# A mean-subtraction kernel on a ring of SBUF slots: blocks of three groups per partition, moved in two DMAs of 50,688 bytes a partition

## The chip, the cores and the metric

The kernel runs on one core of a Trainium2 chip. The metric is the device time of one execution in microseconds (us), lower is better. Each profile below is one execution; its span is about 1.8 us shorter than the time that is measured for it. A run counts as slow when it lies over 1.5% above the fastest of the same kernel.

## The reference

```python
B, S, D = 8, 4096, 2112          # float32
stride = 4
x_r = x.reshape(B, S // stride, stride, D)
pooled = x_r.mean(axis=2)
return x - np.repeat(pooled, stride, axis=1)
```

From every four adjacent rows their mean is subtracted. There are 8192 groups of four rows. A group has 4 x 2112 values, 33,792 bytes, and is contiguous in memory. Every byte must be read once and written once: 553.65 MB in all. That makes the kernel a copy with a little arithmetic in the middle.

## The kernel before

128 groups make a tile, one group in each partition. Six slots in SBUF (the memory on the chip that DMAs fill and engines work on) each hold one tile. SP (the sync engine's queue) issues loads, DVE (the vector engine) does three additions and one multiply-and-add, ACT's queue issues stores. All waits are set by hand on semaphores, counters that a finished DMA or instruction raises. A load into a slot waits only for the store that left that slot six tiles earlier. The words "group" and "tile" are used alike below for these 128 groups: there are 64 of them in the run.

```python
SLOTS = 6
PAD = 224
...
    pad_pool.tile([P, PAD], f32, name="pad")          # 896 bytes, never used
    slots = [io_pool.tile([P, W], f32, name=f"slot{b}") for b in range(SLOTS)]
...
        for k in range(n):                            # n = 64
            b, lap = k % SLOTS, k // SLOTS
            rows = slots[b].rearrange("p (f d) -> p f d", f=STRIDE)
            s = s_ps if k % 2 else s_sb
            tile_rows = slice(k * P, (k + 1) * P)

            load = nc.sync.dma_start(out=slots[b][:], in_=xg[tile_rows])
            if lap:
                load._wait_ge(store_sems[b], 16 * lap)
            load.then_inc(load_sems[b], 16)

            add = nc.vector.tensor_add(out=s[:], in0=rows[:, 0, :], in1=rows[:, 1, :])
            add._wait_ge(load_sems[b], 16 * (lap + 1))
            ...                                       # two more additions, one subtraction
            store = nc.scalar.dma_start(out=og[tile_rows], in_=slots[b][:])
            store._wait_ge(done_sem, done)
            store.then_inc(store_sems[b], 16)
```

Of the kernel before, what the change touches and what calls it, by code (L numbers as in the profile page):

```python
# [1 line left out]

# [4 lines left out]

STRIDE = 4
SLOTS = 6  # L10
PAD = 224


@with_exitstack
def kernel(
    ctx: ExitStack,
    tc: tile.TileContext,
    x: bass.AP,
    out: bass.AP,
):  # L20





    nc = tc.nc
    B, S, D = x.shape
    P = nc.NUM_PARTITIONS
    W = STRIDE * D
    G = (B * S) // STRIDE  # L30
    assert S % STRIDE == 0 and G % P == 0
    n = G // P

    xg = x.rearrange("b (g f) d -> (b g) (f d)", f=STRIDE)
    og = out.rearrange("b (g f) d -> (b g) (f d)", f=STRIDE)
    f32 = mybir.dt.float32

    pad_pool = ctx.enter_context(tc.tile_pool(name="pad", bufs=1))
    io_pool = ctx.enter_context(tc.tile_pool(name="io", bufs=1))
    sum_pool = ctx.enter_context(tc.tile_pool(name="sum", bufs=1))  # L40
    psum_pool = ctx.enter_context(
        tc.tile_pool(name="psum", bufs=1, space=bass.MemoryType.PSUM)
    )
    pad_pool.tile([P, PAD], f32, name="pad")
    slots = [io_pool.tile([P, W], f32, name=f"slot{b}") for b in range(SLOTS)]
    s_sb = sum_pool.tile([P, D], f32, name="s_sb")
    s_ps = psum_pool.tile([P, D], f32, name="s_ps")

    load_sems = [tc.alloc_semaphore(f"load{b}") for b in range(SLOTS)]
    store_sems = [tc.alloc_semaphore(f"store{b}") for b in range(SLOTS)]  # L50
    done_sem = tc.alloc_semaphore("done")

    with tc.tile_critical():  # L53
        done = 0
        for k in range(n):
            b, lap = k % SLOTS, k // SLOTS
            rows = slots[b].rearrange("p (f d) -> p f d", f=STRIDE)
            s = s_ps if k % 2 else s_sb
            tile_rows = slice(k * P, (k + 1) * P)

            load = nc.sync.dma_start(out=slots[b][:], in_=xg[tile_rows])
            if lap:
                load._wait_ge(store_sems[b], 16 * lap)
            load.then_inc(load_sems[b], 16)

            add = nc.vector.tensor_add(out=s[:], in0=rows[:, 0, :], in1=rows[:, 1, :])  # L66
            add._wait_ge(load_sems[b], 16 * (lap + 1))
            add.then_inc(done_sem)
            done += 1
            for f in range(2, STRIDE):  # L70
                add = nc.vector.tensor_add(out=s[:], in0=s[:], in1=rows[:, f, :])  # L71
                add._wait_ge(done_sem, done)
                add.then_inc(done_sem)
                done += 1
            sub = nc.vector.scalar_tensor_tensor(  # L75
                out=rows,
                in0=s[:, None, :].to_broadcast([P, STRIDE, D]),
                scalar=-1.0 / STRIDE,
                in1=rows,
                op0=mybir.AluOpType.mult,  # L80
                op1=mybir.AluOpType.add,
            )
            sub._wait_ge(done_sem, done)
            sub.then_inc(done_sem)
            done += 1

            store = nc.scalar.dma_start(out=og[tile_rows], in_=slots[b][:])
            store._wait_ge(done_sem, done)
            store.then_inc(store_sems[b], 16)

        for b in range(SLOTS):
            nc.sync.wait_ge(store_sems[b], 16 * len(range(b, n, SLOTS)))


# [1 line left out]
_INS = ['x']  # L96
_OUTS = [((8, 4096, 2112), 'float32')]


# [23 lines left out]
```

## Time and profile before

| | kernel before |
|---|---|
| median of 6 runs | 1286.87 us (1286.72 to 1287.26) |
| span of the profiled run | 1285.0 us |
| DVE busy | 1026.5 us, 16.1 us a group |
| data moved | 553.67 MB, mean 431 GB/s |
| DMA packets an engine | 1024 rows of 33,792 bytes |

These are lines of the profile page of the kernel before. The two rows of the second part cut the span into 40 slices: DMA is the busy share of the 16 DMA engines in tenths, GB/s what they moved, loads and stores together.

```profile
span 1285.0 us, 439 instructions
DVE 1026.5 (80%) x256; POOL 0.2 (0%) x4
...
DMA  9999999999999999999999999999999999999998
GB/s 404 421 438 432 426 438 437 430 429 437 437 431 429 437 437 431 429 437 437 431 429 437 437 431 429 437 436 430 430 438 434 429 432 438 434 428 433 438 434 374
DMA packets 18434, 553.67 MB, mean 431 GB/s; under 512 B 2048, under 2 KB 2048, under 8 KB 2048
```

The 2048 small packets, 4 bytes and 9 ns each in the packet records, are 16 for each of 128 DMAs; I take them for the semaphore updates. The view by windows of the same run gives, for each stretch, its length, the busy time of DVE and POOL with the number of their instructions, the clock share, the DMA share and GB/s:

```profile
100.00:500.00 400.00, 321.20 (x81) 0.00 (x0) 1.00 1.00 433
500.00:1150.00 650.00, 523.49 (x130) 0.00 (x0) 1.00 1.00 433
...
1265.00:1270.00 5.00, 4.57 (x1) 0.00 (x0) 1.00 1.00 433
1270.00:1277.00 7.00, 0.00 (x0) 0.00 (x0) 1.00 1.06 459
```

The DMA share is 1.00 in every stretch from 50 to 1270 us (0.98 in the first 50): the engines hardly pause before the end. The view of waits says what DVE waits for (us in total, times, longest):

```profile
DVE s_sb L66 <- DMA slot<-in_x_dram: 123.4, 30, 13.3
DVE s_ps L66 <- DMA slot<-in_x_dram: 113.0, 30, 4.8
```

60 waits, all for loads, 236 us in all. So DMA is the bound and DVE has slack of about 3.8 us a group (16.1 of 19.95 us). The timeline has the last arithmetic:

```profile
1253.41 2.37 DVE L66 TENSOR_TENSOR s_ps<-slot 128x2112 f32<-128x2112 f32 x1 [3.82 <-DMA slot<-in_x_dram]
1255.81 4.77 DVE L71 TENSOR_TENSOR s_ps<-s_ps,slot 128x2112 f32<-128x2112 f32 x2
1260.61 8.96 DVE L75 SCALAR_TENSOR_TENSOR slot<-s_ps,slot 128x8448 f32<-128x8448 f32 x1
```

The last store leaves at 1269.6 us. At that time the engines are still writing the store before it, which lands at 1273.4 us. There is no gap.

### The profile page before, as it was taken

The page shows a single profiled execution, that of the slowest core. Times are in us where ns is not written, and L with a number is a line of the kernel's source. Part 1 is how long each engine was busy: PE and PEld are TensorE (multiplying, and loading weights), DVE is VectorE, ACT ScalarE, POOL GpSimd, SP SyncE. Part 2 cuts the span into 40 slices and gives each one's busy share as a digit, 9 for nine tenths or more (in the row PEclk, how much of TensorE's full clock was granted, in tenths as well). Part 3 has the DMA queues.
Part 4 walks back from the last instruction along what each step waited for, and adds up shares of the span by engine and source line. Part 5 has one row for each costly group of instructions (what it writes and reads, how often), then busy time and mean ns, then how long its engine had stood idle before and what let it go on. Part 6 is the DMA issues. An engine that isn't in the chain of part 4 may idle for free.

```text
span 1285.0 us, 439 instructions
## 1 busy us (share of the span) xinstructions
DVE 1026.5 (80%) x256; POOL 0.2 (0%) x4
## 2 busy tenths in 40 slices
DVE  5998778787787877878778788787887878878774
POOL 0000000000000000000000000000000000000000
DMA  9999999999999999999999999999999999999998
GB/s 404 421 438 432 426 438 437 430 429 437 437 431 429 437 437 431 429 437 437 431 429 437 437 431 429 437 436 430 430 438 434 429 432 438 434 428 433 438 434 374
DMA packets 18434, 553.67 MB, mean 431 GB/s; under 512 B 2048, under 2 KB 2048, under 8 KB 2048
## 3 DMA queue, kind: packets, MB, share of 16 engines
q1 hardware_dynamic: 9216, 276.83, 50.0%
q10 hardware_dynamic: 9216, 276.83, 49.9%
q14 instruction: 2, 0.02, 0.0%
HBM read 276.82 MB, written 276.82 MB: 431 GB/s over the span
## 4 chain that ended last, share of the span: by engine, by line
DVE 80%; another core or an unknown queue 17%; DMA 1%; issue 0%; SPq 0%
DVE slot L75 45%; DVE s_ps L71 12%; DVE s_sb L71 12%; DVE s_ps L66 6%; DVE s_sb L66 6%; DMA slot<-in_x_dram 1%; SPq L118 0%; SPq L53 0%
## 5 line engine op out<-in xcount | busy, mean ns | idle before, releaser
L75 DVE SCALAR_TENSOR_TENSOR slot<-s_sb,slot 128x8448 f32<-128x8448 f32 x32 | 286.7, 8958 | 1.1
L75 DVE SCALAR_TENSOR_TENSOR slot<-s_ps,slot 128x8448 f32<-128x8448 f32 x32 | 286.6, 8957 | 1.1
L66 DVE TENSOR_TENSOR s_sb<-slot 128x2112 f32<-128x2112 f32 x32 | 75.5, 2358 | 123.4 <-DMA slot<-in_x_dram 123.4
L66 DVE TENSOR_TENSOR s_ps<-slot 128x2112 f32<-128x2112 f32 x32 | 75.7, 2367 | 113.0 <-DMA slot<-in_x_dram 113.0
L71 DVE TENSOR_TENSOR s_ps<-s_ps,slot 128x2112 f32<-128x2112 f32 x64 | 151.4, 2366 | 2.2
L71 DVE TENSOR_TENSOR s_sb<-s_sb,slot 128x2112 f32<-128x2112 f32 x64 | 150.9, 2358 | 2.2
L107 POOL MEMSET const-uint8-127<- 128x1 uint8 x1 | 0.1, 102 | 0.0
L107 POOL MEMSET const-bfloat16-1.0<- 128x1 bf16 x1 | 0.1, 101 | 0.0
L107 POOL MEMSET const-float32-0.0<- 128x1 f32 x1 | 0.1, 98 | 0.2 <-issue 0.2
L107 POOL MEMSET const-float32-1.0<- 128x1 f32 x1 | 0.1, 98 | 0.0
## 6 DMA issues: line engine op xcount, KB each, us to landing
slot<-in_x_dram SPq DMA_DIRECT2D x64, 4224.0 KB, 59.7
out_dram<-slot ACTq DMA_DIRECT2D x64, 4224.0 KB, 43.9
```

Source lines behind the costliest of these rows:

```text
L66: add = nc.vector.tensor_add(out=s[:], in0=rows[:, 0, :], in1=rows[:, 1, :])
L71: add = nc.vector.tensor_add(out=s[:], in0=s[:], in1=rows[:, f, :])
L75: sub = nc.vector.scalar_tensor_tensor(out=rows, in0=s[:, None, :].to_broadcast([P, STRIDE, D]), scalar=-1.0 / STRIDE, in1=rows, op0=mybir ...
L107: nc = _bacc.Bacc("TRN2", target_bir_lowering=False, num_devices=1)
```

## The change

The intent: fewer and larger DMA packets. A partition now owns three adjacent groups, 101,376 contiguous bytes, moved as two DMAs of 50,688 bytes a partition. The six slots become one ring that holds two such blocks. 20 blocks of three are followed by four single groups. The pad tile goes. Eight semaphores a side serve in turn. The core of the diff:

```diff
-SLOTS = 6
-PAD = 224
+RING = 6
+SUPER = 3
+TAIL = 4
+SEMS = 8
...
+    blocks = [SUPER] * ((n - TAIL) // SUPER)
+    blocks += [1] * (n - sum(blocks))
+    for k in blocks:
+        src = xg[rows].rearrange("(p j) w -> p (j w)", j=k)
+        dst = og[rows].rearrange("(p j) w -> p (j w)", j=k)
+        parts = 1 if k == 1 else 2
+        step = k * W // parts
+        for h in range(parts):
+            ...  # moves: ring columns, source, destination, last group that the move holds
+        for j in range(k):
+            ...  # groups: ring column, last move that must have landed
-    pad_pool.tile([P, PAD], f32, name="pad")
-    slots = [io_pool.tile([P, W], f32, name=f"slot{b}") for b in range(SLOTS)]
+    ring = io_pool.tile([P, RING * W], f32, name="ring")
...
+        for i, (a, b, src, _, _) in enumerate(moves):
+            taken = ...  # stores whose ring columns this load overwrites
+            load = nc.sync.dma_start(out=ring[:, a:b], in_=src)
+            for m in taken[-1:]:
+                load._wait_ge(*landed(store_sems, m))
...
+            while stored < len(moves) and moves[stored][4] <= j:
+                a, b, _, dst, _ = moves[stored]
+                store = nc.scalar.dma_start(out=dst, in_=ring[:, a:b])
```

Two things follow. The middle group of a block lies in both halves, so the first half can be stored only after the second half has landed and two groups are done. And the ring now has four pieces in flight instead of six.

More of the change, by code (lines that the diff above doesn't have):

```diff
@@ L30 @@
     G = (B * S) // STRIDE
-    assert S % STRIDE == 0 and G % P == 0
+    assert S % STRIDE == 0 and G % P == 0 and (SUPER * W) % 2 == 0
     n = G // P
+    f32 = mybir.dt.float32
     xg = x.rearrange("b (g f) d -> (b g) (f d)", f=STRIDE)
     og = out.rearrange("b (g f) d -> (b g) (f d)", f=STRIDE)
-    f32 = mybir.dt.float32
-    pad_pool = ctx.enter_context(tc.tile_pool(name="pad", bufs=1))
+    blocks = [SUPER] * ((n - TAIL) // SUPER)
+    blocks += [1] * (n - sum(blocks))
+    moves = []
+    groups = []
+    slot = g0 = 0
+    for k in blocks:
+        assert slot + k <= RING
+        rows = slice(g0, g0 + k * P)
+        src = xg[rows].rearrange("(p j) w -> p (j w)", j=k)
+        dst = og[rows].rearrange("(p j) w -> p (j w)", j=k)
+        parts = 1 if k == 1 else 2
+        step = k * W // parts
+        first_move, first_group = len(moves), len(groups)
+        for h in range(parts):
+            part = slice(h * step, (h + 1) * step)
+            a = slot * W + h * step
+            last = first_group + ((h + 1) * step - 1) // W
+            moves.append((a, a + step, src[:, part], dst[:, part], last))
+        for j in range(k):
+            groups.append(((slot + j) * W, first_move + ((j + 1) * W - 1) // step))
+        g0 += k * P
+        slot = (slot + k) % RING
     io_pool = ctx.enter_context(tc.tile_pool(name="io", bufs=1))
@@ L43, with landed @@
     )
-    pad_pool.tile([P, PAD], f32, name="pad")
-    slots = [io_pool.tile([P, W], f32, name=f"slot{b}") for b in range(SLOTS)]
+    ring = io_pool.tile([P, RING * W], f32, name="ring")
     s_sb = sum_pool.tile([P, D], f32, name="s_sb")
     s_ps = psum_pool.tile([P, D], f32, name="s_ps")
-    load_sems = [tc.alloc_semaphore(f"load{b}") for b in range(SLOTS)]
-    store_sems = [tc.alloc_semaphore(f"store{b}") for b in range(SLOTS)]
+    load_sems = [tc.alloc_semaphore(f"load{i}") for i in range(SEMS)]
+    store_sems = [tc.alloc_semaphore(f"store{i}") for i in range(SEMS)]
     done_sem = tc.alloc_semaphore("done")
+    def landed(sems, i):
+        return sems[i % SEMS], 16 * (i // SEMS + 1)
     with tc.tile_critical():
-        done = 0
-        for k in range(n):
-            b, lap = k % SLOTS, k // SLOTS
-            rows = slots[b].rearrange("p (f d) -> p f d", f=STRIDE)
-            s = s_ps if k % 2 else s_sb
-            tile_rows = slice(k * P, (k + 1) * P)
-            load = nc.sync.dma_start(out=slots[b][:], in_=xg[tile_rows])
-            if lap:
-                load._wait_ge(store_sems[b], 16 * lap)
-            load.then_inc(load_sems[b], 16)
+        owner = {}
+        free = set()
+        for i, (a, b, src, _, _) in enumerate(moves):
+            taken = sorted(
+                {m for (p, q), m in owner.items() if p < b and a < q} - free
+            )
+            for m in taken[:-1]:
+                nc.sync.wait_ge(*landed(store_sems, m))
+            load = nc.sync.dma_start(out=ring[:, a:b], in_=src)
+            for m in taken[-1:]:
+                load._wait_ge(*landed(store_sems, m))
+            load.then_inc(load_sems[i % SEMS], 16)
+            free.update(taken)
+            owner = {c: m for c, m in owner.items() if m not in free}
+            owner[(a, b)] = i
+        done = 0
+        seen = -1
+        stored = 0
+        for j, (c, need) in enumerate(groups):
+            rows = ring[:, c:c + W].rearrange("p (f d) -> p f d", f=STRIDE)
+            s = s_ps if j % 2 else s_sb
             add = nc.vector.tensor_add(out=s[:], in0=rows[:, 0, :], in1=rows[:, 1, :])
-            add._wait_ge(load_sems[b], 16 * (lap + 1))
+            assert need <= seen + 1
+            if need > seen:
+                add._wait_ge(*landed(load_sems, need))
+                seen = need
             add.then_inc(done_sem)
@@ L85 @@
             done += 1
-            store = nc.scalar.dma_start(out=og[tile_rows], in_=slots[b][:])
-            store._wait_ge(done_sem, done)
-            store.then_inc(store_sems[b], 16)
-        for b in range(SLOTS):
-            nc.sync.wait_ge(store_sems[b], 16 * len(range(b, n, SLOTS)))
+            while stored < len(moves) and moves[stored][4] <= j:
+                a, b, _, dst, _ = moves[stored]
+                store = nc.scalar.dma_start(out=dst, in_=ring[:, a:b])
+                store._wait_ge(done_sem, done)
+                store.then_inc(store_sems[stored % SEMS], 16)
+                stored += 1
+        assert stored == len(moves)
+        for m in sorted(set(range(len(moves))) - free):
+            nc.sync.wait_ge(*landed(store_sems, m))
 _INS = ['x']
```

## The prediction

> **What bounds the kernel now: the 16 DMA engines, throughout.** The page shows a span of 1285.0 us (timed: 1286.73), DVE busy 1026.5 us (80%), and 553.67 MB at a mean of 431 GB/s. The view by windows gives 433 GB/s and a DMA share of 1.00 from 50 to 1260 us. The view of waits has DVE waiting 236 us for loads, for nothing else. The trace's packet records sharpen this: a packet is one partition's row of 33,792 bytes; rows follow each other every 1247.8 ns on each engine without a gap, from about 1.95 to 1281.5 us. 1024 rows x 1.2478 us = 1278 us: that is the kernel; some 2 us at each end are the rest. The chain of waits names DVE for 80%, but DVE works 16.1 us of each 19.95 us, so it is not the bound.
>
> [...]
>
> **What the change does.**
> - Removes: data packets per engine fall from 1024 to 704 (640 of 50,688 bytes), DMAs from 128 to 88. [...] about 0.4 us of semaphore packets (9 ns each). [...]
> - Adds, silently: the pad tile is gone. In the built programs the slots began at an SBUF address that is a multiple of 512; the ring and all its moves begin 128 bytes past one. [...]
> - Moves: the first addition starts near 18 us instead of 13.3; the first store leaves only after group 1, near 50 us instead of 29.5. Six groups of loads keep the engines busy until about 60 us, so this costs nothing. DVE work is the same 256 instructions.
> - Tail: before, the last store was issued at 1269.6 us with about 2 us of backlog. A small queue model fitted to the trace gives an idle gap of 0 to 3 us just before the last single store; I count 1 us.
> - Middle: loads are issued in bursts, but the model always keeps work in one of the two queues.
>
> **Sum:** [...] All of it is on the critical path, which is the DMA engines.
>
> **Prediction: 1286.0 us, 8 in 10 between 1283.0 and 1291.0. Chances: faster by over 2% 0.01, within 2% 0.94, slower by over 2% 0.05.**
>
> **What would show it.** 11,264 data packets[...]. DMA share 1.00 in the middle; any drop near 1270 us only. DVE busy unchanged, with fewer, longer waits for loads.
>
> **What would make it wrong.** [...] Landings later than modelled would empty both queues once per block and cost 10 to 30 us.

The forecast's sum came to +0.9 us over the timed 1286.73: -0.4 for the semaphore packets, +1 for the tail, and two terms, a saving by fewer data packets and the cost of the start address ("alignment" below), which came to about +0.3 together. For doubt of the second it was then shaded down to 1286.0.

## The result, and the profile after

The changed kernel took 1289.56 us (median of 6: 1290.40, 1286.27, 1286.33, 1288.72, 1292.78, 1293.20). The kernel before took 1286.87. The ratio of the fast runs is 1.0021, with a 95% interval of 0.9999 to 1.0042: the same. Ratios here are the mean time of one kernel's fast runs over the mean of the other's in the same rounds, so they are not quite the ratio of the medians. The new thing is the spread: 7 us, against 0.5 us before. The profiled run is the one of 1290.40 us. Its page:

```profile
span 1288.6 us, 398 instructions
DVE 1023.0 (79%) x256; POOL 0.2 (0%) x4
...
DMA  9999999999999999999999999999999999999997
GB/s 403 428 428 434 439 436 428 428 439 437 431 430 434 441 433 428 433 439 434 431 431 439 436 431 430 437 438 431 430 434 442 431 430 431 437 437 425 429 428 325
DMA packets 12674, 553.67 MB, mean 430 GB/s; under 512 B 1408, under 2 KB 1408, under 8 KB 1408
```

Its waits and its windows:

```profile
DVE s_sb L103 <- DMA ring<-in_x_dram: 132.0, 11, 18.8
DVE s_ps L103 <- DMA ring<-in_x_dram: 114.3, 11, 12.4
```

```profile
50.00:100.00 50.00, 49.69 (x14) 0.00 (x0) 1.00 1.00 424
100.00:500.00 400.00, 318.76 (x80) 0.00 (x0) 1.00 1.00 434
500.00:1150.00 650.00, 527.12 (x132) 0.00 (x0) 1.00 1.00 434
...
1265.00:1270.00 5.00, 4.97 (x2) 0.00 (x0) 1.00 1.00 433
1270.00:1277.00 7.00, 5.83 (x1) 0.00 (x0) 1.00 0.28 121
```

The packets are fewer, as intended, and the middle runs at 434 instead of 433 GB/s. But between 1270 and 1277 us the engines are busy for 28% of the time only, where before they were full. The timeline shows why:

```profile
1259.67 2.37 DVE L103 TENSOR_TENSOR s_ps<-ring 128x2112 f32<-128x2112 f32 x1 [4.18 <-DMA ring<-in_x_dram]
...
1266.87 8.96 DVE L115 SCALAR_TENSOR_TENSOR ring<-s_ps,ring 128x8448 f32<-128x8448 f32 x1
```

The last addition starts 6.3 us later than before, so the last store leaves at 1275.9 instead of 1269.6 us, after 15 of the 16 engines have run out of work.

The trace also records when each of the 16 engines reports its part of a DMA. The last load is told done by its first engine at 1252.9 us, by its 15th at 1254.9 us and by its last at 1259.6 us. In the kernel before these were 1251.6, 1252.2 and 1253.4. So one engine of 16 held the last group back: the code waits for all 16 counts, and DVE's addition starts at 1259.67 us, after the 16th report and not after the 15th. The price is the 4.7 us between the last engine and the one before it. By an estimate from the packet records, the gaps before the last store, 5.7 us an engine in the mean, would shrink to about 1.3 us if it had left these 4.7 us earlier. I call the time from the first to the last engine of one DMA its landing spread.

Where did that straggler come from? The fourth load from the end, issued at 1154.4 us and the first of a single group, is reported by 15 engines between 1180.2 and 1181.7 us, and by the last at 1187.3 us. These are the starts in us of the rows that two engines served, from the packet records (L a row of this load, S a row of a store, e the semaphore packet that ends this load):

```
one of the 15   S 1174.98  L 1176.85  L 1178.10  L 1179.35  e 1180.59  S 1180.60  S 1182.47
the straggler   S 1174.11  L 1175.98  S 1177.22  L 1179.09  L 1180.35  S 1181.97  L 1183.84  S 1185.09  e 1186.96
```

The straggler still had one row of the old store to write and so was a little behind, with two load rows left when the rows of the next store (issued at 1178.0 us) came in. From there it served the two queues in turn: one store row, 1.87 us, went before its last load row, and one more between that row and the semaphore packet. (In the kernel before, load and store rows alternate in 96% or more of neighbouring packets from 120 to 1200 us; the exact share depends on how packets are put into chains.) So a lag of under 2 us became one of 5.6 us by order alone. The records do not name engines, but here the chain is certain: the row at 1183.84 is the 128th and last of this load, and no row of the next load starts before 1184.37. That the arrival of the store decided this order is my reading of the records; the order and the times are in them.

### The profile page after: what moved, and what is told of

Its sections match the earlier page's. It is cut to its first block, busy times and chain, and to the rows that moved or that the text cites. A ratio compares the mean times of both kernels' runs of the same rounds, so it can differ in the third digit from the quotient of the medians.

```text
span 1288.6 us, 398 instructions
## 1 busy us (share of the span) xinstructions
DVE 1023.0 (79%) x256; POOL 0.2 (0%) x4
## 4 chain that ended last, share of the span: by engine, by line
DMA 66%; DVE 27%; another core or an unknown queue 6%; issue 0%; SPq 0%
DMA out_dram<-ring 35%; DMA ring<-in_x_dram 30%; DVE ring L115 15%; DVE s_ps L111 4%; DVE s_sb L111 4%; DVE s_ps L103 2%; DVE s_sb L103 2%; SPq L89 0%; SPq L161 0%; SPq L80 0%
## 5 line engine op out<-in xcount | busy, mean ns | idle before, releaser
L115 DVE SCALAR_TENSOR_TENSOR ring<-s_sb,ring 128x8448 f32<-128x8448 f32 x32 | 286.7, 8958 | 1.1
L115 DVE SCALAR_TENSOR_TENSOR ring<-s_ps,ring 128x8448 f32<-128x8448 f32 x32 | 286.6, 8957 | 1.1
L103 DVE TENSOR_TENSOR s_sb<-ring 128x2112 f32<-128x2112 f32 x32 | 75.2, 2351 | 132.0 <-DMA ring<-in_x_dram 132.0
L103 DVE TENSOR_TENSOR s_ps<-ring 128x2112 f32<-128x2112 f32 x32 | 75.6, 2362 | 114.3 <-DMA ring<-in_x_dram 114.3
L111 DVE TENSOR_TENSOR s_ps<-s_ps,ring 128x2112 f32<-128x2112 f32 x64 | 151.4, 2366 | 2.2
L111 DVE TENSOR_TENSOR s_sb<-s_sb,ring 128x2112 f32<-128x2112 f32 x64 | 150.9, 2358 | 2.2
```

Of the source, the lines that this page charges most:

```text
L111: add = nc.vector.tensor_add(out=s[:], in0=s[:], in1=rows[:, f, :])
L115: sub = nc.vector.scalar_tensor_tensor(out=rows, in0=s[:, None, :].to_broadcast([P, STRIDE, D]), scalar=-1.0 / STRIDE, in1=rows, op0=mybir ...
```

## The experiments

Two sums are used below, both from the packet records and both given per engine. *Stretch* is what packets took beyond the usual duration of their size (1251 ns for 33,792 bytes, 1872 ns for 50,688). *Gaps* is time between two packets of an engine. A stretched packet counts as busy, so the DMA share stays at 1.00 and only GB/s shows it (e6 has 395 GB/s at a share of 1.01 from 50 to 100 us). The records do not name the engine; I put packets into 16 chains by end and start, so single chains can be mixed up, the sums hardly. With a limit of 2% every version here counts as the same as the kernel before; smaller differences are read from the ratios of fast runs (95% intervals in brackets). The experiments ran in three batches on three chips (e1 to e4, e5 to e8, e9 to e12), each with the kernel before beside it, which was 1286.8 to 1286.9 us on all three. The changed kernel itself was not run again, so versions of it from different batches were never timed side by side.

### e1 and e2: alignment alone

The pad was put back into the changed kernel (e1) and taken out of the kernel before (e2).

```diff
 # e1, on the changed kernel
+    pad_pool = ctx.enter_context(tc.tile_pool(name="pad", bufs=1))
+    pad_pool.tile([P, 224], f32, name="pad")
     ring = io_pool.tile([P, RING * W], f32, name="ring")
 # e2, on the kernel before
-    pad_pool.tile([P, PAD], f32, name="pad")
```

> The changed kernel with the 896-byte pad put back, so that every DMA starts at an SBUF address that is a multiple of 512 again; nothing else differs. [...] If alignment is free, the packets stay at 1868 to 1869 ns and the times lie where those of the changed kernel lie, 1286 to 1293, with the same spread.

> The kernel before without its pad, so that its slots start 128 bytes past a multiple of 512. [...] If it is free: 1286.7 to 1287.3 as before, rows every 1247 to 1248 ns, and the pad did nothing.

"Free" means that the start address makes no difference.

e2: 1286.78 us (1286.63 to 1286.94), ratio 0.9999 [0.9987, 1.0011]; rows follow each other 1247 ns apart in most cases, as before. e1: 1291.55 us (1288.28 to 1297.20); 1868 ns, as in the changed kernel. So a start 128 bytes past a multiple of 512 (by the built programs; the traces hold no addresses) costs nothing here: the spacings are the same, and 1286.78 us stand against 1286.82 with the pad. The cost that the prediction gave it was an estimate that no trace showed, and it was wrong. e1 is also a second draw of the changed kernel's behaviour: its ratio to the kernel before is 1.0040 [1.0021, 1.0060], and its profile (1289.7 us) has such a gap before the last store too (5.4 us an engine) and one late engine on the last load (15th at 1254.4, last at 1259.0 us).

### e3 and e4: the last subtraction and store cut in four

```diff
+            if j == len(groups) - 1:
+                for f in range(STRIDE):
+                    sub = nc.vector.scalar_tensor_tensor(
+                        out=rows[:, f, :], in0=s[:], in1=rows[:, f, :], ...)
+                    store = nc.scalar.dma_start(
+                        out=dst[:, f * D:(f + 1) * D], in_=rows[:, f, :])
```

> The changed kernel with the last group's subtraction cut into four row-wise pieces and a store after each. Theory (an empty DMA backlog before the last store): the gap of 6.4 us before the last store nearly closes, since the first piece of the store can leave about 6.7 us earlier; the time falls to about 1285 and the spread between runs (1286.3 to 1293.2) shrinks to 1 to 2 us. Rival (the loss lies in the middle, or in skewed engines whatever the tail does): the times and the spread stay as they are, less at most 1 us.

> Control: the same cut of the last group in the kernel before. There the last store is issued while about 2 us of backlog stand in the engines, so the theory expects no gain: within 0.5 us of 1286.9. If splitting the store helps by itself (shorter last store, earlier receipt), this gains as much as the changed kernel does, several us.

e4, the control: 1286.90 us (1286.86 to 1287.00), no gain, as expected of a kernel with a backlog at its end. e3: 1290.48 us (1286.17 to 1299.34). The expectation failed in its main point: the spread did not shrink (one run of six, 1299.34 us, makes most of it). The profile fell on the best run (1286.17 us). There the last load landed within 3.0 us on all engines, and there was no gap:

```profile
1265.00:1270.00 5.00, 4.93 (x3) 0.00 (x0) 1.00 0.93 400
1270.00:1277.00 7.00, 0.97 (x1) 0.00 (x0) 1.00 1.00 425
```

Because that load came in time, this run does not test whether the cut closes a gap. A run of 1299 us probably lost its time elsewhere. That is what the next experiments look for.

### e5: one single group at the end instead of four

```diff
-TAIL = 4
+TAIL = 1
```

> The changed kernel with one single group at the end instead of four (21 blocks of three). If the loss and the spread come from the passage from blocks to four single groups (a slow engine's single load landed 5.6 us behind the others there, and the last addition waits for it), this runs at 1284 to 1287 with a spread of 2 us or less. If they come from the big blocks themselves (few, large, bursty moves anywhere in the run), it spreads as the changed kernel does, 1286 to 1293, or more, since the last-but-one store is larger.

1286.20 us (1285.26 to 1289.19), ratio 0.9998 [0.9984, 1.0012]. This is the lowest median of the changed family. Three of five runs are faster than any run of the kernel before, but the spread is 4 us, not 2, so neither branch of the expectation fits whole. In the profiled run (1287.75 us) the last load's landing spread is 6.7 us and 2.4 us of gaps are left.

### e6: faster arithmetic, wrong results on purpose

```diff
-            for f in range(2, STRIDE):
+            for f in range(2, 2):
```

> The changed kernel with two of the three additions left out in every group, so wrong results on purpose: DVE needs 11.3 us a group instead of 16.1, all DMAs are the same. If the loss is the time that the last groups' arithmetic leaves the engines without work (empty queues before the last store), it shrinks: about 1284 to 1287 and no gap over 3 us before the last store. If the loss lies in the DMAs themselves (order of packets, slow engines), the times stay 1286 to 1293.

Fast runs: 1290.95, 1292.38 and 1310.01 us, ratio 1.0085 [1.0026, 1.0145]; a fourth, 1320.10 us, is slow. That is slower than the kernel before. It is not shown to be slower than the changed kernel, in whose range (up to 1293.20 us) two of the three lie. The windows of the profiled run (1292.38 us):

```profile
50.00:100.00 50.00, 33.73 (x7) 0.00 (x0) 1.00 1.01 395
...
1270.00:1277.00 7.00, 4.28 (x1) 0.00 (x0) 1.00 0.97 420
```

The gap before the last store is gone (share 0.97 instead of 0.28), as the theory of the tail says. But from 50 to 100 us the engines move 395 GB/s at a share of 1.01: they look full and are not. The packet records of that window have stores that take 0.3 to 0.7 us and loads that take up to 1.8 us longer than usual, 4.6 us an engine in all. So in this run the tail is cured and more is lost elsewhere. That the faster DVE does it, by changing when stores are issued and so how the two queues meet, is my guess; no run tested it.

### e7 and e8: slower arithmetic

One addition more in every group, into the sum buffer not in use; DVE then needs 18.4 us a group, still less than the 19.95 us of DMA.

```diff
+            spare = s_sb if j % 2 else s_ps
+            add = nc.vector.tensor_add(out=spare[:], in0=rows[:, 0, :], in1=rows[:, 1, :])
```

> The changed kernel with one addition more (2.4 us) in every group, into the sum buffer not in use: DVE 18.4 us a group, still under the 19.9 us of DMA. If the changed kernel has lost the slack that the one before had, it slows by 3 us or more, with gaps at the end and perhaps once per block; if it has slack, by at most 1 us.

> The kernel before with the same extra addition in every group. Theory: six independent single slots keep stores queued, so it stays within 1 us of 1286.9. Rival: both kernels lose alike, 3 us or more.

e7, fast runs: 1295.71 and 1297.68 us, ratio 1.0077 [1.0058, 1.0095]; two more, 1319.48 and 1324.33 us, are slow. e8: 1293.94 us (1292.70 to 1295.24), ratio 1.0055 [1.0042, 1.0069]. The mean of e7's fast runs is 7.1 us above that of the changed kernel, the mean of e8 7.1 us above that of the kernel before. So the expectation for e8 (within 1 us) failed, and the rival it named held: both lose alike. Only slow runs would make the changed kernel the more sensitive one, and they cannot be used for that. In e8 the windows show where:

```profile
500.00:1150.00 650.00, 595.72 (x164) 0.00 (x0) 1.00 1.00 433
1265.00:1270.00 5.00, 4.93 (x3) 0.00 (x0) 1.00 1.00 433
1270.00:1277.00 7.00, 7.00 (x1) 0.00 (x0) 1.00 0.17 72
```

The middle is untouched at 433 GB/s. All is lost in the gap before the last store, as in the profile of the changed kernel: gaps are 6.8 us an engine longer than in the kernel before, of a slowdown of 7.0 us in the profiled run. The last load is reported by its first engine at 1249.0, its 15th at 1251.8 and its last at 1259.1 us. The last store leaves at 1277.7 us, 8.1 us later than in the kernel before; 2.4 us of that are the added addition and 5.7 us the later landing. So with less slack the kernel before has a late engine too, and has it long before the end: the landing spread is 6.4 us at 600 us and 9.0 us at 1000 us, and costs nothing there (433 GB/s). Less slack goes with more spread here, but slack alone does not decide: e6 had more of it and was not faster.

In e7's profile (1295.7 us) stretch is 7.9 us and gaps are 4.5 us above those of the kernel before. The first stretch begins after a load and a store were issued 0.9 us apart (165.6 and 166.5 us), the store into a queue that had nothing left.

### e9: the candidate

e5 and e3 together.

> The changed kernel with one single group at the end and its last subtraction and store cut in four: the candidate to beat both. With one single group alone the profile had a gap of 1.8 us at the end and 0.6 us before it; with the cut they should vanish: 1284.7 to 1286.5, under the kernel before's 1286.8 in most runs. If a queue that runs dry in the middle is what makes the spread, single runs still reach 1288 or more.

1296.14 us (1290.76 to 1300.80), ratio 1.0067 [1.0048, 1.0086]: worse than e5; against e3 (1.0035 [1.0011, 1.0060]) the intervals overlap. In its profile (1290.8 us) the last load needs from 1240.2 us (first engine) to 1251.4 us (last; the 15th at 1242.6), and 2.5 us an engine of gaps lie between 1200 and 1250 us. The two parts do not add, and this version beats neither kernel. Its program differs from e5's only in its last group, yet its profile has the larger landing spread at 1150 us already (5.5 against 4.1 us), so part of the difference is the luck of the draw. Another part may be the chip: e5 ran on one, e9 on another. How much I cannot say.

### e10: twice as many packets, in the kernel before

```diff
+            for h in range(2):
+                part = slice(h * half, (h + 1) * half)
+                load = nc.sync.dma_start(out=slots[b][:, part], in_=xg[tile_rows, part])
```

(and the same for the stores)

> The kernel before with every load and store cut into two DMAs of 16,896 bytes a partition, 2048 packets an engine instead of 1024. The spacings of 1247 and 1868 ns for 33,792 and 50,688 bytes give, by a straight line, 5.0 ns fixed per packet and 27.2 bytes a ns. If that is right, packets follow each other every 626 ns, and the run takes 5.1 us more for them and about 1.2 us for 128 more semaphore packets: 1292 to 1294. If the cost goes with bytes: every 623.5 ns, and 1287 to 1288.5.

1292.29 us (1292.00 to 1292.36), 5.5 us more than before, ratio 1.0043 [1.0028, 1.0057], with packets 626 ns apart in most cases. So a packet has a fixed cost here. (Less 1.2 us for 128 more semaphore packets, the 5.5 us give 4.2 ns for each of 1024 more packets.) The usual spacings of three sizes lie on a line: 16,896 bytes 626 ns, 33,792 bytes 1247 ns, 50,688 bytes 1868 ns, that is 621 ns for each 16,896 bytes and 5 ns for the packet. The premise of the change is right: an engine goes from 1024 packets to 704 and saves 1.6 us, and 40 fewer DMAs save 40 semaphore packets of 9 ns, 0.4 us.

### e11 and e12: the program of e3, profiled again

Same program as e3; two more draws, to catch a long run.

> The same program as the changed kernel with the cut last group, once more, to profile one of its slow runs (1289 to 1299; the first profile fell on a run of 1286). Theory: a slow run shows no gap over 1 us before the last store, but packets stretched for tens of us somewhere, after a store or load queue had run empty and was started again, adding up to what the run is slower. Rival: a gap at the end after all.

> As the second look; one more draw of the same program. Each slow run is expected to have its own place of stretched packets or its own gap; a fast run (under 1287) is expected to have neither beyond the first 100 us.

Both fell on long runs: 1299.56 us and 1291.88 us. The windows of e11:

```profile
100.00:500.00 400.00, 318.81 (x80) 0.00 (x0) 1.00 1.00 433
500.00:1150.00 650.00, 516.81 (x131) 0.00 (x0) 1.00 1.00 429
1150.00:1200.00 50.00, 37.57 (x10) 0.00 (x0) 1.00 0.96 404
```

From 500 us on the rate falls to 429 GB/s at a share of 1.00, and at 1150 to 1200 us there are real gaps. Before the last store there is hardly any gap. The landing times of one load in the middle, in us, of the same program's good run (e3), of this one, and of the kernel before:

```
                 first engine   15th engine   last engine
kernel before        952.1         952.7         954.0
e3 (1286.2 us)       949.6         951.5         951.7
e11 (1299.6 us)      950.1         951.3         962.0
```

In e11 15 engines agree within 1.2 us and one is 10.7 us late. The next load or the next store waits for that engine, and the others run their store queue empty: ten times from 585 to 1129 us a store is issued when only 2 rows, of 16 engines, are left of the stores before it. In the 12 us after nine of these, packets are stretched, by 0.24 to 0.80 us an engine. After the tenth (888 us), and after two earlier stores that met the same (463 and 523 us), they are not (0.07 us or less). Other profiles are as mixed: a store that met an empty queue near 1180 us was followed by 1.12 us of stretch in e12, 0.08 in the changed kernel and 0.03 in e9. So an emptied queue goes with stretching in this run; it is not shown to cause it. The landing spread of this run grew step by step: 2.2 us for the load issued last before 200 us, 5.9 at 600 us, 11.5 at 1000 us. In e3, the same program, it stayed at 1.9, 2.0 and 2.1 us. In the kernel before it was 1.0, 0.9 and 1.8 us. e12 has 1.7, 5.4 and 7.4 us, and loses 1.2 us of stretch and 1.0 us of gaps an engine between 1150 and 1200 us.

### The ledger

Each profiled run against the profiled run of the kernel before (1286.81 us), in us. Packets is the saving worked out above (none for e8; the few small packets of the cut stores, 0.1 us, are left out). Stretch and gaps are means over 16 engines, while the run ends with its last engine; "last" is how far the end of that engine lies behind the mean end, against the same in the kernel before (1.5 us).

| run | packets | stretch | gaps | last | sum | measured |
|---|---|---|---|---|---|---|
| changed | -2.0 | +1.3 | +5.7 | -1.4 | +3.6 | +3.6 |
| e1 | -2.0 | +1.1 | +5.3 | -1.4 | +3.0 | +2.9 |
| e3 | -2.0 | +0.5 | 0.0 | +0.8 | -0.7 | -0.6 |
| e5 | -2.1 | +0.9 | +2.3 | -0.1 | +1.0 | +0.9 |
| e6 | -2.0 | +7.3 | 0.0 | +0.3 | +5.6 | +5.6 |
| e7 | -2.0 | +7.9 | +4.5 | -1.4 | +9.0 | +8.9 |
| e8 | 0 | +0.4 | +6.8 | -0.2 | +7.0 | +7.0 |
| e9 | -2.1 | +1.4 | +3.4 | +1.2 | +3.9 | +4.0 |
| e11 | -2.0 | +8.2 | +3.3 | +3.0 | +12.5 | +12.8 |
| e12 | -2.0 | +2.9 | +1.1 | +2.9 | +4.9 | +5.1 |

The terms account for every profiled run within 0.3 us. They say where the time went, not why packets were stretched or engines fell behind.

## Why the prediction was right or wrong

The time (1286.0 predicted, 1289.56 measured, range 1283 to 1291) and "within 2%" held for the median; two of the six runs lie above the range. Part of this is luck. The range of 8 us is hardly wider than the kernel's own spread of 7 us; the alignment cost, too high by its whole amount, and the tail, too low by more than that, partly cancel; and e1, the same program but for the pad, had its median at 1291.55 us, outside the range. The shading from the sum (1286.73 + 0.9 is 1287.6) down to 1286.0 doubted the alignment cost with reason, but moved the total away from what was measured.

- **The bound.** Right. The DMA share is 1.00 from 100 to 1150 us in every profiled run of the changed family, and in the changed kernel 433 became 434 GB/s. Full is not the same as fast: 427 GB/s in e7 from 100 to 500 us and 429 in e11 from 500 us on, at the same share.
- **Packets.** A saving was forecast, and there is one: 5 ns for each data packet, shown by three sizes (e10), and 9 ns for each semaphore packet, 2.0 us in all. When it was forecast, the part for data packets was an estimate that no trace showed.
- **Alignment.** Wrong: a cost was forecast, and it is 0 (e1, e2). Rows follow each other every 1247 and 1868 ns with the pad and without it. The step that failed is the assumed cost of the start address, which had no trace behind it.
- **Start.** Right: first addition at 18.8 us (said: near 18), first store at 51.0 (near 50), engines not idle.
- **Tail, +1 us.** An idle gap before the last store was foreseen, but sized too small: 5.7 us in the profiled run. The model took all 16 engines as one. The 15th engine had landed the last load at 1254.9 us; the last one took until 1259.6. Without these 4.7 us the gap is about 1.3 us by the estimate above, close to what was said, so what the prediction lacked is the late engine.
- **Middle, "the model always keeps work in one of the two queues".** Not so in bad runs: e11 has 3.4 us of gaps between 1150 and 1200 us. And even where work is there, packets are stretched (8.2 us in e11, 7.3 in e6), which the model did not have.
- **"What would make it wrong": late landings would cost 10 to 30 us.** By amount, the worst fast runs of e3 (1299.34) and e6 (1310.01 us) are like this. In e11, a profiled bad run, it is one late engine rather than all. The worst runs of e6 and e7 were not profiled.

What stays open: why a single engine falls so far behind in some runs and not in others of the same program, and what stretches packets. All fourteen profiles have some stretch, 0.6 to 1.2 us an engine in the 12 us after the first store was issued (0.85 in the kernel before, 1.02 in the changed kernel), and e7 has 3.9 us an engine between 150 and 200 us. Nor is it known which part of the change brings the spread: larger packets, four pieces in flight instead of six, or the first half's wait for the second. No run changed one of these alone. An engine may lose 0.5 us to a hiccup (two single load rows took 0.54 us longer in the kernel before, at 206 and 846 us), which the kernel before absorbs. That such a hiccup seeds the late engine is plausible, not shown. No run tested it, and the long runs of the changed kernel itself, which were not profiled (1292.8 and 1293.2 us), are explained only by analogy.

No version beat both kernels clear of noise. e5 is level with the kernel before and has the fastest single run (1285.26 us).

## What to carry to other kernels

With the DMA engines full (share 1.00), a small saving per packet was real here and can be computed from two packet spacings (2 us of 1287), but it must be set against what late engines cost (4.7 us at the end of the changed kernel's profile). My guess, not tested part by part, is that larger pieces, fewer of them, and stores that wait for two pieces make each DMA's slowest engine everyone's engine. Look at the landing spread and at GB/s beside the busy share, not at the busy share alone. And time several runs: here the median moved by 0.2%, but the spread went from 0.5 to 7 us.
